# Layer-norm boundaries of an encoder trunk: the work of GpSimd handed to VectorE, tile by tile

## The chip, the cores and the metric

The kernel runs on one core of a Trainium2 chip. The metric is the device time of one execution in microseconds (us). TensorE (PE in the profile) multiplies matrices, with PEld for its weight loads; VectorE (DVE), ScalarE (ACT) and GpSimd (POOL) do elementwise work, each in the order of its own queue; SyncE (SP) issues all transfers.

## What is computed

The reference is a trunk of two layers on a sequence of 512 tokens of width 1024. Layer 0 mixes with gated linear attention, layer 1 with softmax attention; each layer then has an MLP of width 4096 with squared ReLU. After each of the four sub-layers stands the step that this document is about:

```
u = x * (1.0 + sc1) + sh1
y = gla_mixer(u, ...)                     # or chunk_attention, or squared_relu_mlp
x = layer_norm(DEEPNORM_ALPHA * x + (1.0 + g1) * y, ln_g[i, 0], ln_b[i, 0])
...
def layer_norm(x, g, b):
    mu = jnp.mean(xf, -1, keepdims=True)
    var = jnp.mean(jnp.square(xf - mu), -1, keepdims=True)
    return ((xf - mu) * lax.rsqrt(var + LN_EPS)) * g + b
```

`sh`, `sc` and `g` come from a conditioning vector and are columns per feature.

## The kernel before

Activations lie with features on the 128 partitions and tokens along the row: `xs[0..7]` are eight tiles of 128 features by 512 tokens, in fp32. Every large product is done with operands split in two (`hi`, rounded, and `lo`, the remainder `raw - hi`), three matmuls for one (`mm3`). ScalarE casts `hi`, and `lo_of` makes the remainder: 128x1024 for a weight tile (`emit_unit`), on VectorE for weights of kind `w` and `f`, on GpSimd for kinds `p` and `F`. There are two `p` tiles (one in each MLP) and two `F` tiles (first MLP weights of layer 1). `fill` and `fill_f` emit these units from a list `plan`; they take their places in the queues where they are emitted. All operations of one engine keep the order in which the program emits them (class `InOrder`), so each queue is an order written by hand. Line 47 is the helper that records every operation, so all rows of the trace name that line and groups are told apart by their tiles.

`boundary(...)` ends a sub-layer. It is called four times: after the linear attention (first), after the MLP of layer 0 (second, with `vfill`: the product behind it is the value projection of the attention), after the attention (third, in which the events hold no `"shift"`; called late here), and after the last MLP (fourth, `final`, which writes the output). Its stages:

1. Output tiles 0 to 3 of the sub-layer's last product are finished on all 512 tokens and evicted into `xs` (`ev`). A rough mean of the tokens (`shift_mm`, a matmul with `ones_h`, and a copy by ScalarE) is subtracted from all eight tiles, to keep the sum of squares small. In the first, second and fourth boundaries this lies ahead of the last tile; in the third behind the first half of tile 4.
2. `start_acc` sums tiles 0 to 3 in `accz` and their squares in `accq`.
3. Tiles 4 to 7 are computed in two halves of 256 tokens: `half_mm` is eight steps of three matmuls of 128x256; `half_ev` evicts, squares on ScalarE and adds to `accz` and `accq`. The order on TensorE is the first half of tiles 4 to 7, then the second half of tile 4 (in the third boundary also three steps of tile 5), then the statistics of the first half, then the rest.
4. `stats1` multiplies the sums by `ones_c` (which gives mean and mean square on all partitions), forms the variance, and centres the tiles; `stats2` finishes the inverse root `y`.
5. `ap1` scales a pair of tiles by `y` and applies the affine columns of the next sub-layer twice, once rounded (`un`, part 0) and once in fp32 (`us`); `ap2` makes the remainder (`un`, part 1). In the last boundary `norm` and `affine` do this and the output transfers follow.
6. The next product (`fg` with four weight tiles, or `v_mm`) goes through its eight steps, one for each tile of `un`, first half and then second half. The statistics of the second half stand behind the first two steps (three in the third boundary).

Between VectorE and GpSimd the elementwise work is shared so:

```
for j in (4, 5, 6, 7):
    if j > 5 or "shift" in events:
        tt(G, xs[j], xs[j], shift, ALU.subtract)
...
for k in (1, 3, 5, 7):
    tt(G, xs[k][:, hs], xs[k][:, hs], mn, ALU.subtract)
...
for k in (1, 3, 7) if final and hf else (1, 3, 5, 7):
    tt(G, xs[k][:, hs], xs[k][:, hs], y, ALU.mult)
```

GpSimd also adds most of the squares and makes the affine columns `a1`, `b1`, `ag`, `ab` (`ln_cols`).

Of the kernel before, what the change touches and what calls it, by code (L numbers as in the profile page):

```python
# [59 lines left out]
def trunk(ctx, tc, xT, c, ada, cols, gk1, gk2, w_qk, w_v, w_g, w_go, a_qk, a_v, a_tab,  # L60
# [128 lines left out]
    def emit_unit():  # L189
# [26 lines left out]
        lo_of(G if kind in "pF" else V, lo, raw, hi)  # L216
# [90 lines left out]
    def ln_cols(l, i, nxt):  # L307
# [4 lines left out]
        if nxt is not None:  # L312
            nl, sh, sc = nxt
            mS = mods[:, nl, sc * 8:sc * 8 + 8]
            mH = mods[:, nl, sh * 8:sh * 8 + 8]
            a1 = const.tile([P, 8], F32, name=nm("a1"))
            b1 = const.tile([P, 8], F32, name=nm("b1"))
            tt(G, a1, g, mS, ALU.mult)
            tt(G, b1, b, mS, ALU.mult)
            tt(G, b1, b1, mH, ALU.add)  # L320
            ag = const.tile([P, 8], F32, name=nm("ag"))
            ab = const.tile([P, 8], F32, name=nm("ab"))
            G.tensor_scalar(out=ag, in0=g, scalar1=ALPHA, scalar2=None, op0=ALU.mult)
            G.tensor_scalar(out=ab, in0=b, scalar1=ALPHA, scalar2=None, op0=ALU.mult)
            r.update(a=a1, b1=b1, ag=ag, ab=ab)
# [4 lines left out]
    def boundary(src, l, gt, open_lnt, mk_cols, fg_evac, events=None, final=False, vfill=None):  # L330
# [25 lines left out]
        def ev(m):  # L356
            stt(xs[m], pss[m], mod(l, gt, m), xs[m], ALU.mult, ALU.add)
            if m == 1:
                tt(V, accz, xs[0], xs[1], ALU.add)

        def shift_mm():
            pm = bank()
            T.matmul(pm, ones_h, accz, start=True, stop=True)
            A.copy(out=shift, in_=pm)
            for j in (4, 5, 6, 7):
                if j > 5 or "shift" in events:
                    tt(G, xs[j], xs[j], shift, ALU.subtract)
                else:
                    tt(V, xs[j], xs[j], shift, ALU.subtract)
            for j in (0, 1):  # L370
                tt(V, xs[j], xs[j], shift, ALU.subtract)

        events = events or [(0, range(8)), (1, range(8)), (2, range(8)), "shift", (3, range(8))]
        late = "shift" not in events
        for e in events:
            if e == "shift":
                shift_mm()
                continue
# [5 lines left out]
            if left[m] == 0:  # L384
                ev(m)
                if m < 3 and "shift" in events:
                    fill(3)
        lnc = mk_cols()
# [3 lines left out]
        def start_acc():  # L392
            for m in (2, 3):
                tt(V, xs[m], xs[m], shift, ALU.subtract)
            tt(V, accz, xs[0], xs[1], ALU.add)
            A.activation(out=accq, in_=xs[0], func=AF.Square)
            tt(G if "shift" in events else V, accq, accq, sq_of(xs[1], S), ALU.add)
            for m in (2, 3):
                tt(V, accz, accz, xs[m], ALU.add)
                if late and m == 3:  # L400
                    q = shift
                    A.activation(out=q, in_=xs[m], func=AF.Square)
                else:
                    q = sq_of(xs[m], S)
                tt(G, accq, accq, q, ALU.add)

        if "shift" in events:
            start_acc()
        else:
            fill_f(4)  # L410
# [6 lines left out]
        def half_ev(m, hf, ps, j, mid=lambda: None):  # L417
            hs = slice(hf * HT, (hf + 1) * HT)
            xh = xs[m][:, hs]
            stt(xh, ps[:, j * HT:(j + 1) * HT], mod(l, gt, m), xh, ALU.mult, ALU.add)  # L420
# [5 lines left out]
            tt(V if m == 7 or (final and hf) else G, accq[:, hs], accq[:, hs], q, ALU.add)  # L426
# [6 lines left out]
        def stats1(hf, last=None, fill_in=None):  # L433
# [13 lines left out]
            mn = tl("mn", 1)  # L447
            A.copy(out=mn, in_=dm)
            ve = tl("ve", 1)
            stt(ve, qm, LN_EPS, d2, ALU.add, ALU.subtract)  # L450
            tt(V, xs[0][:, hs], xs[0][:, hs], dm, ALU.subtract)
            for k in (1, 3, 5, 7):
                tt(G, xs[k][:, hs], xs[k][:, hs], mn, ALU.subtract)
# [4 lines left out]
            for k in (2, 4):  # L458
                tt(V, xs[k][:, hs], xs[k][:, hs], dm, ALU.subtract)
            st[hf] = dm, ve, y0  # L460

        def stats2(hf):
            hs = slice(hf * HT, (hf + 1) * HT)
# [3 lines left out]
            tt(V, xs[6][:, hs], xs[6][:, hs], dm, ALU.subtract)  # L467
# [3 lines left out]
            st[hf] = y  # L471
            for k in (1, 3, 7) if final and hf else (1, 3, 5, 7):
                tt(G, xs[k][:, hs], xs[k][:, hs], y, ALU.mult)
# [4 lines left out]
        def ap1(hf, p):  # L478
            ks = (2 * p, 2 * p + 1)
            hs = slice(hf * HT, (hf + 1) * HT)  # L480
            k = ks[0]
            tt(V, xs[k][:, hs], xs[k][:, hs], st[hf], ALU.mult)
            for k in ks:
                xh = xs[k][:, hs]
                a1, b1 = lnc["a"][:, k:k + 1], lnc["b1"][:, k:k + 1]
                us[k] = tl("u", 4)
                A.activation(out=un[k][:, 0, hs], in_=xh, func=AF.Identity, scale=a1, bias=b1)
                if k % 2:
                    V.tensor_scalar(out=us[k], in0=xh, scalar1=a1, scalar2=b1, op0=ALU.mult, op1=ALU.add)
                else:  # L490
                    A.activation(out=us[k], in_=xh, func=AF.Identity, scale=a1, bias=b1)

        def ap2(hf, p):
            hs = slice(hf * HT, (hf + 1) * HT)
            for k in (2 * p, 2 * p + 1):
                lo_of(V, un[k][:, 1, hs], us[k], un[k][:, 0, hs])

        def norm(hf, k):
            hs = slice(hf * HT, (hf + 1) * HT)
            tt(V, xs[k][:, hs], xs[k][:, hs], st[hf], ALU.mult)  # L500
# [20 lines left out]
        for m in range(4, 8):  # L521
            pa[m] = bank()
            half_mm(m, 0, pa[m], 0)
            if m == 4 and "shift" not in events:
                shift_mm()
                start_acc()
            half_ev(m, 0, pa[m], 0)
        pb = {m: bank() for m in range(4, 8)}
        half_mm(4, 1, pb[4], 0)
        if late:  # L530
            half_mm(5, 1, pb[5], 0, range(3))
            half_ev(4, 1, pb[4], 0)
            stats1(0)
            half_mm(5, 1, pb[5], 0, range(3, KT))
            stats2(0)
        else:
            stats1(0)
            stats2(0)
# [759 lines left out]
```

## Time and profile before

| | |
|---|---|
| median of three runs | 1222.27 us (1222.24 to 1222.6) |
| the profiled execution | 1222.72 us, of which the span of the instructions is 1220.9 us |
| TensorE busy | 1181.6 us, 97% of the span |
| VectorE busy | 831.1 us, 68% |
| ScalarE busy | 544.8 us, 45% |
| GpSimd busy | 176.6 us, 14% |
| mean granted clock of TensorE | 0.990 |
| share of the chain that ended last | TensorE 77%, VectorE 13%, ScalarE 4%, GpSimd 3% |

Matmuls are pipelined and their ends are modelled, so a busy TensorE is not one at its peak; the waits ahead of its instructions say more. In the timelines a row has the start, the time from the start of the first to the end of the last of the merged instructions, the engine, the operation with its output and inputs, their number, and in brackets how long the engine was idle before it and what ended that. A granted clock of 1.00 is 2.4 GHz, 0.50 is 1.2 GHz.

### The profile page before, as it was taken

Reading aid. Unit: us, or ns where it says so; the run is one execution under the profiler, and the core shown is the slowest. Engines: PE = TensorE matmul, PEld = TensorE weight load, DVE = VectorE, ACT = ScalarE, POOL = GpSimd, SP = SyncE. Lnnn points to the kernel's source line nnn. Section 1 sums busy time; section 2 is a strip of 40 time slices with the busy share of each in tenths; the row PEclk is TensorE's granted clock in tenths of the full one; section 3 lists DMA queues with packets and bytes.
Section 4 is the critical chain, followed back from the end, with each engine's and each line's share of the span. In section 5 each row is a group of like instructions: output and inputs, shape, how many; then the busy total and the mean of one; then the engine's idle time right before and its main releaser. Section 6 shows DMA issues by size and latency. Waiting matters only on the chain.

```text
span 1220.9 us, 15202 instructions
## 1 busy us (share of the span) xinstructions
PE 1181.6 (97%) x5742; PEld 985.9 (81%) x5742; DVE 831.1 (68%) x1260; ACT 544.8 (45%) x853; POOL 176.6 (14%) x189
## 2 busy tenths in 40 slices
PE   9999999899999999999899999998999999999995
PEld 5888888788888888888788786678888888888885
DVE  6788589777676677658834878898764443443467
ACT  4564545474243342342536656654641422322324
POOL 1000003610000000005511222235200000000035
PEclk9999999999999999999999999999899999999998
DMA  9756435028889889844026431321155232332201
GB/s 350 257 187 218 170 104 188 3 76 306 291 302 344 295 301 336 297 157 156 31 74 224 155 118 63 130 85 55 62 196 152 90 104 86 102 105 88 94 10 69
DMA packets 58282, 196.33 MB, mean 161 GB/s; under 512 B 6561, under 2 KB 10913, under 8 KB 58210
## 3 DMA queue, kind: packets, MB, share of 16 engines
q1 hardware_dynamic: 58210, 195.37, 46.1%
q8 instruction: 45, 0.74, 0.2%
q14 instruction: 27, 0.22, 0.1%
HBM read 174.37 MB, written 20.97 MB: 160 GB/s over the span
## 4 chain that ended last, share of the span: by engine, by line
PE 77%; DVE 13%; ACT 4%; POOL 3%; issue 2%; ACTq 0%; DVEq 0%; POOLq 0%
PE ps L47 76%; DVE af L47 5%; DVE x L47 3%; ACT af L47 2%; DVE ar L47 2%; POOL af L47 1%; DVE u L47 1%; POOL x L47 1%; DVE wlo L47 1%; PE warm L47 1%; ACT ar L47 1%; DVE d L47 1%; DVE y L47 1%; DVE t L47 0%; DVE raw L47 0%
## 5 line engine op out<-in xcount | busy, mean ns | idle before, releaser
L47 PE MATMUL ps<-ar,whi 128*128 128x512 f32 (+1 forms) x2880 | 822.1, 373 | 0.2 <-DVE ar L47 0.2
L47 PEld LDWEIGHTS ps<-ar,whi 128*128 128x128 f32 x2880 | 526.7, 190 | 96.4 <-issue 2.4
L47 PE MATMUL ps<-ar,wlo 128*128 128x512 f32 (+1 forms) x1440 | 526.0, 372 | 0.2 <-DVE wlo L47 0.2
L47 PEld LDWEIGHTS ps<-ar,wlo 128*128 128x128 f32 x1440 | 273.3, 190 | 46.9 <-DVE wlo L47 0.8
L47 ACT CAST whi<-raw 128x1024 fp32r<-128x1024 f32 (+1 forms) x169 | 169.5, 1010 | 204.8 <-PE ps L47 168.6
L47 DVE TENSOR_TENSOR wlo<-raw,whi 128x1024 fp32r<-128x1024 f32 x160 | 200.2, 1256 | 20.9 <-ACT whi L47 19.1
L47 DVE SCALAR_TENSOR_TENSOR x<-ps,mods,x 128x512 f32<-128x512 f32 (+1 forms) x96 | 63.0, 657 | 123.1 <-PE ps L47 123.1
L47 POOL TENSOR_TENSOR x<-x,af 128x512 f32<-128x512 f32 x14 | 25.4, 1843 | 808.7 <-ACT af L47 808.7
L47 DVE TENSOR_TENSOR h<-r 128x512 f32<-128x512 f32 (+1 forms) x72 | 49.2, 688 | 85.5 <-ACT r L47 84.7
L47 ACT ACTIVATE r<-ps 128x512 f32<-128x512 f32 (+1 forms) x72 | 39.1, 549 | 133.0 <-PE ps L47 132.8
L47 DVE SCALAR_TENSOR_TENSOR raw<-raw,csil 128x1024 f32<-128x1024 f32 x80 | 96.8, 1217 | 0.0
L47 PE MATMUL ps<-ar,fhi 128*128 128x256 f32 (+1 forms) x320 | 70.9, 317 | 6.8 <-DVE ar L47 5.9
L47 DVE TENSOR_TENSOR ar<-h,ar 128x512 fp32r<-128x512 f32 (+1 forms) x72 | 45.6, 633 | 39.5 <-ACT ar L47 38.4
L47 ACT CAST ar<-h 128x512 fp32r<-128x512 f32 (+1 forms) x72 | 41.2, 572 | 51.0 <-DVE h L47 51.0
L47 PEld LDWEIGHTS ps<-ar,fhi 128*128 128x128 f32 x320 | 53.9, 198 | 10.6 <-DVE ar L47 7.1
L47 PE MATMUL ps<-whi,ar 128*128 128x512 f32 x192 | 60.6, 390 | 0.0
L47 POOL PARTITION_ALL_REDUCE mb<-af x16 | 31.7, 1984 | 131.0 <-DVE af L47 123.9
L47 PE MATMUL ps<-ar,flo 128*128 128x256 f32 (+1 forms) x160 | 49.9, 312 | 0.0
L47 ACT ACTIVATE af<-x 128x256 f32<-128x256 f32 (+1 forms) x48 | 22.7, 486 | 57.6 <-POOL af L47 31.8
L47 PEld LDWEIGHTS ps<-whi,ar 128*128 128x128 f32 x192 | 36.0, 188 | 7.6
L47 ACT CAST fhi<-raw 128x1024 fp32r<-128x1024 f32 x30 | 31.4, 1049 | 23.7 <-DMA raw<-a_qk 12.2
L47 ACT ACTIVATE af<-af 128x1024 f32<-128x1024 f32 (+2 forms) x48 | 32.0, 698 | 20.9 <-DVE af L47 20.4
(149 smaller groups left out, 1139.4 us busy)
## 6 DMA issues: line engine op xcount, KB each, us to landing
raw<-f SPq DMA_DIRECT2D x128, 512.0 KB, 4.3
raw<-ada SPq DMA_DIRECT2D x80, 512.0 KB, 4.6
hraw<-ada SPq DMA_DIRECT2D x16, 512.0 KB, 9.0
raw<-a_qk SPq DMA_DIRECT2D x16, 512.0 KB, 5.4
khi_q<-fhi SPq DMA_DIRECT2D x14, 512.0 KB, 3.6
klo_q<-flo SPq DMA_DIRECT2D x14, 512.0 KB, 4.9
whi<-khi_q SPq DMA_DIRECT2D x14, 512.0 KB, 3.3
wlo<-klo_q SPq DMA_DIRECT2D x14, 512.0 KB, 4.3
```

The lines of the kernel that those rows point to most:

```text
L47: r = f(*a, **k)
```

## The change

All elementwise work of the boundaries goes to VectorE, and the orders are rewritten.

- The four weight remainders of kinds `p` and `F`, and the affine columns, go to VectorE; the columns are made at the start of `boundary` instead of behind its events.
- The shift is taken from tile 0 alone, twice its value, instead of from tiles 0 and 1; the sum of the two drops out of the evictions. In the third boundary the shift's product moves ahead of the last steps of tile 3, and the subtractions stay late: tiles 4 and 0 to 3 before the eviction of tile 4, the others each before its own.
- In the other three, tiles 4 to 7 and 0 to 2 are shifted before the eviction of tile 3, and tile 3 after it.
- `accq` is summed on VectorE throughout, with the squares of ScalarE in two buffers (one in the third boundary).
- The copy `mn` of the mean to SBUF drops out; all centring reads the mean from PSUM (`cen`). In the three inner boundaries the first statistics stand in the middle of the eviction of tile 4's second half, in the third without the three steps of tile 5 ahead of them.
- Centring, scaling, affine pieces and remainders are emitted one tile after the other (`cen`, `ap`, `lo`) instead of in pairs; the fp32 affine piece of the odd tiles moves from VectorE to ScalarE.
- The statistics of the second half stand behind three steps of the next product everywhere. In the second boundary the four weight tiles of the value projection's other half are all made after the first half's work.

```diff
-        lo_of(G if kind in "pF" else V, lo, raw, hi)
+        lo_of(V, lo, raw, hi)
...
-            tt(G, a1, g, mS, ALU.mult)
+            tt(V, a1, g, mS, ALU.mult)
...
+        lnc = mk_cols()
...
-            T.matmul(pm, ones_h, accz, start=True, stop=True)
-            A.copy(out=shift, in_=pm)
+            T.matmul(pm, ones_h, xs[0], start=True, stop=True)
+            A.activation(out=shift, in_=pm, func=AF.Copy, scale=2.0)
...
             if e == "shift":
                 shift_mm()
+                if not late:
+                    sub(4, 5, 6, 7, 0, 1, 2)
...
             A.activation(out=accq, in_=xs[0], func=AF.Square)
+            q = [shs[:, 1, :], shs[:, 1 if late else 0, :]]
+            for m in (1, 2, 3):
+                A.activation(out=q[m % 2], in_=xs[m], func=AF.Square)
+                tt(V, accz, xs[0] if m == 1 else accz, xs[m], ALU.add)
+                tt(V, accq, accq, q[m % 2], ALU.add)
...
+            if late:
+                if m == 4:
+                    sub(4, 0, 1, 2, 3)
+                    start_acc()
+                else:
+                    sub(m)
+            half_ev(m, 0, pa[m])
...
+        def ap(hf, *ks):
             hs = slice(hf * HT, (hf + 1) * HT)
             for k in ks:
                 xh = xs[k][:, hs]
                 a1, b1 = lnc["a"][:, k:k + 1], lnc["b1"][:, k:k + 1]
                 us[k] = tl("u", 4)
+                tt(V, xh, xh, st[hf][1], ALU.mult)
                 A.activation(out=un[k][:, 0, hs], in_=xh, func=AF.Identity, scale=a1, bias=b1)
+                A.activation(out=us[k], in_=xh, func=AF.Identity, scale=a1, bias=b1)
...
+        half_ev(4, 1, pb[4], lambda: stats1(0, 2))
+        stats2(0)
+        half_mm(5, 1, pb[5], 0)
+        ap(0, 0, 1)
+        lo(0, 0)
+        half_ev(5, 1, pb[5])
+        cen(0, 2, 3)
+        ap(0, 2)
+        lo(0, 1)
...
+        def second():
+            ap(0, 5)
+            lo(0, 4)
+            stats1(1, 2)
+            cen(0, 6, 7)
+            ap(0, 6)
+            lo(0, 5)
+            stats2(1)
+            ap(0, 7)
+            lo(0, 6, 7)
+
+        def third():
+            ap(1, 0, 1)
+            for k in range(2, KT):
+                cen(1, k)
+                ap(1, k)
+                lo(1, k - 2)
+            lo(1, KT - 2, KT - 1)
```

In the last boundary the order is rewritten likewise, with a centring and a scaling in front of each affine piece:

```diff
+            norm(1, 3)
+            affine(1, 3, (3, 6))
+            cen(1, 4)
             norm(1, 4)
             affine(1, 4, (4, 5))
+            cen(1, 5)
             norm(1, 5)
             affine(1, 5, (4, 5))
+            cen(1, 6)
             norm(1, 6)
-            affine(1, 3, (3, 6), True)
             affine(1, 6, (3, 6), True)
+            cen(1, 7)
+            norm(1, 7)
             affine(1, 7, (7,))
```

## Rows read from the trace of the kernel before

**Rows 1.** Waits of TensorE: us in total, times, longest.

```profile
PE ps L47 <- DVE af L47: 12.6, 9, 3.8
PE ps L47 <- DVE ar L47: 9.3, 8, 2.3
```

**Rows 2.** Timeline of TensorE, first boundary.

```profile
218.74 0.70 PE L47 MATMUL ps<-af,ones_c 128*128 128x256 f32 x2 [0.54 <-DVE af L47]
223.24 1.22 PE L47 MATMUL ps<-af,ones_c 128*128 128x256 f32 x2 [3.81 <-DVE af L47]
...
249.78 0.39 PE L47 MATMUL ps<-ar,fhi 128*128 128x256 f32 x1 [1.56 <-DVE ar L47]
...
261.27 0.63 PE L47 MATMUL ps<-ar,whi 128*128 128x512 f32 x2
```

**Rows 3.** Stretches: busy us (x instructions) by engine, granted clock, DMA share, GB/s.

```profile
core 0: us, PE busy (x) PEld busy (x) DVE busy (x) ACT busy (x) POOL busy (x), PEclk, DMA share, GB/s
223.24:226.20 2.96, 2.96 (x12) 2.78 (x13) 1.02 (x4) 1.18 (x4) 0.97 (x2) 0.50 0.01 3
584.20:588.00 3.80, 3.80 (x17) 3.69 (x18) 2.24 (x7) 1.48 (x4) 2.19 (x3) 0.55 0.00 0
...
249.80:255.80 6.00, 6.00 (x50) 6.00 (x51) 4.82 (x12) 5.03 (x10) 1.29 (x1) 1.00 0.01 3
861.80:867.80 6.00, 6.00 (x28) 6.00 (x29) 4.83 (x12) 5.03 (x10) 1.29 (x1) 0.50 0.00 0
```

**Rows 4.** Groups by shape: busy us, mean ns of one; idle before, releaser.

```profile
L47 POOL TENSOR_TENSOR x<-x,mn 128x256 f32<-128x256 f32 x32 | 25.6, 829 | 26.0 <-ACT mn L47 26.0
...
L47 DVE TENSOR_TENSOR mods<-mods,col 128x8 f32<-128x8 f32 x8 | 1.3, 167 | 0.3
```

**Rows 5.** Timeline of VectorE, first boundary.

```profile
210.75 1.29 DVE L47 TENSOR_TENSOR x<-x,af 128x512 f32<-128x512 f32 x2
...
215.47 0.47 DVE L47 SCALAR_TENSOR_TENSOR x<-ps,mods,x 128x256 f32<-128x256 f32 x1
215.97 0.42 DVE L47 TENSOR_TENSOR af<-af,x 128x256 f32<-128x256 f32 x1
...
229.81 0.95 DVE L47 TENSOR_TENSOR x<-x,y 128x256 f32<-128x256 f32 x1
...
249.98 0.41 DVE L47 TENSOR_TENSOR x<-x,y 128x256 f32<-128x256 f32 x1
250.32 0.40 DVE L47 TENSOR_SCALAR u<-x,a,b 128x256 f32<-128x256 f32 x1
```

**Rows 6.** Timeline of ScalarE, first boundary.

```profile
201.09 0.59 ACT L47 COPY af<-ps 128x512 f32<-128x512 f32 x1 [0.46 <-PE ps L47]
...
251.43 1.08 ACT L47 ACTIVATE ar<-x,b,a 128x256 fp32r<-128x256 f32 x2
```

**Rows 7.** Timeline of VectorE, second boundary.

```profile
562.51 2.32 DVE L47 TENSOR_TENSOR wlo<-raw,whi 128x1024 fp32r<-128x1024 f32 x1
```

**Rows 8.** Timeline of TensorE, second boundary.

```profile
582.35 0.70 PE L47 MATMUL ps<-af,ones_c 128*128 128x256 f32 x2 [0.96 <-DVE af L47]
584.19 0.85 PE L47 MATMUL ps<-af,ones_c 128*128 128x256 f32 x2 [1.15 <-DVE af L47]
...
629.87 0.39 PE L47 MATMUL ps<-whi,ar 128*128 128x512 f32 x1
```

**Rows 9.** Timeline of VectorE, ahead of the third boundary's half tiles.

```profile
809.18 3.50 DVE L47 TENSOR_TENSOR wlo<-raw,whi 128x1024 fp32r<-128x1024 f32 x3
...
818.00 1.40 DVE L47 SCALAR_TENSOR_TENSOR x<-ps,mods,x 128x512 f32<-128x512 f32 x2
```

**Rows 10.** Timeline of TensorE, third boundary.

```profile
835.51 0.70 PE L47 MATMUL ps<-af,ones_c 128*128 128x256 f32 x2 [2.99 <-DVE af L47]
...
861.78 0.58 PE L47 MATMUL ps<-ar,fhi 128*128 128x256 f32 x1 [2.34 <-DVE ar L47]
...
875.96 0.63 PE L47 MATMUL ps<-ar,whi 128*128 128x512 f32 x2
```

**Rows 11.** Timeline of SyncE's queue, end of the kernel.

```profile
1217.48 0.45 SPq L516 DMA_DIRECT2D out<-af  x1
```

More of the change, by code (lines that the diff above doesn't have):

```diff
@@ L385, in boundary @@
                 ev(m)
-                if m < 3 and "shift" in events:
+                if m < 3 and not late:
                     fill(3)
-        lnc = mk_cols()
         lnt = open_lnt()
@@ L392, in start_acc @@
         def start_acc():
-            for m in (2, 3):
-                tt(V, xs[m], xs[m], shift, ALU.subtract)
-            tt(V, accz, xs[0], xs[1], ALU.add)
             A.activation(out=accq, in_=xs[0], func=AF.Square)
[L397 to L407, printed above, removed]
+            q = [shs[:, 1, :], shs[:, 1 if late else 0, :]]
[4 more added lines that the diff above has]
+        if late:
+            fill_f(4)
+        else:
+            sub(3)
             start_acc()
-        else:
-            fill_f(4)
         def half_mm(m, hf, ps, j, ks=range(KT)):
@@ L431, in tl, with cen, stats1 @@
             return lnt.tile([P, HT], F32, tag=tag, bufs=bufs, name=nm(tag))
-        def stats1(hf, last=None, fill_in=None):
+        def cen(hf, *ks):
+            hs = slice(hf * HT, (hf + 1) * HT)
+            for k in ks:
+                tt(V, xs[k][:, hs], xs[k][:, hs], st[hf][0], ALU.subtract)
+        def stats1(hf, n0, last=None, fill_in=None):
             hs = slice(hf * HT, (hf + 1) * HT)
@@ L523, in boundary @@
             half_mm(m, 0, pa[m], 0)
[L524 to L527, printed above, removed]
+            if late:
+                if m == 4:
+                    sub(4, 0, 1, 2, 3)
+                    start_acc()
+                else:
+                    sub(m)
+            half_ev(m, 0, pa[m])
         pb = {m: bank() for m in range(4, 8)}
         half_mm(4, 1, pb[4], 0)
[L530 to L534, printed above, removed]
+        if final:
+            stats1(0, 4)
             stats2(0)
[L536 to L539 removed]
+            half_ev(4, 1, pb[4], lambda: norm(0, 0))
             half_mm(5, 1, pb[5], 0)
[L541 removed]
+            affine(0, 0, (0, 2))
+            cen(0, 4, 5)
+            norm(0, 1)
             affine(0, 1, (1, 3))
[L543 to L544 removed]
+            half_ev(5, 1, pb[5], lambda: norm(0, 2))
             half_mm(6, 1, pb[6], 0)
+            affine(0, 2, (0, 2))
+            norm(0, 3)
             affine(0, 3, (1, 3))
[L547 to L548 removed]
+            cen(0, 6, 7)
+            half_ev(6, 1, pb[6], lambda: norm(0, 5))
             half_mm(7, 1, pb[7], 0)
             affine(0, 5, (5, 7))
+            norm(0, 7)
+            affine(0, 7, (5, 7))
             def fill_in():
@@ L622, in boundary @@
             fg(0, fa, range(n))
-            ap1(0, 3)
-            ap2(0, 2)
-            stats1(1)
-            ap2(0, 3)
-            stats2(1)
-            fg(0, fa, range(n, 8))
-            ap1(1, 0)
-            for p in range(1, 4):
-                ap1(1, p)
-                ap2(1, p - 1)
-            ap2(1, 3)
+            second()
+            fg(0, fa, range(n, 8))
+            third()
             fb = [bank(), bank()]
@@ L1241, in trunk @@
     evac_h, run = mlp_fns()
-    u = boundary(o, 1, G1, opener(es, 1), lambda: ln_cols(1, 0, (1, SH2, SC2)), evac_h, ev)
+    u = boundary(o, 1, G1, opener(es, 1), lambda: ln_cols(1, 0, (1, SH2, SC2)), evac_h, ev, late=True)
     hs = run(u, 1)
```

108 lines of the change are left out of this document (33 added, 75 removed).

## The prediction, made before the changed kernel was run

> **What bounds the kernel now.** I read the waits of TensorE first, then TensorE's timeline through the four boundaries (first about 190 to 262 us, second 562 to 630, third 813 to 876, last 1175 to the end), then VectorE, ScalarE and GpSimd in the same stretches. Outside the boundaries TensorE issues without a gap worth naming; all its waits on VectorE together are 12.6 and 9.3 us [rows 1], so the change has to earn its time there. In the first boundary TensorE has nothing left after 218.2 (218.74 less its wait) but the two statistics products and what depends on them: it waits 0.54 us for the sum, then 3.81 us for the sum of squares, later 1.56 us for the first tile of the second half, and leaves the boundary at 261.27 [rows 2]. The long wait costs twice: up to 226.20 the granted clock is 0.50, the lower level of 1.2 GHz, where it is 1.00 from 249.80 on; after the 2.34 us wait of the third boundary it is 0.50 from 861.80 to 867.80, six microseconds at half rate [rows 3, 10].
>
> Who is late? GpSimd takes 829 ns for a subtraction on 256 columns [rows 4]; VectorE does such a piece in 0.41 us and starts the next 0.34 us after it (249.98 to 250.32), and two pieces of 512 columns in 1.29 us, so one every 0.61 [rows 5]. While GpSimd runs, VectorE is slowed as well: the multiplication that has 0.41 us at 249.98 has 0.95 us at 229.81, and the next instruction starts 0.87 later [rows 5]; a 1024-column remainder has 2.32 us at 562.51 against three in 3.50 us at 809.18 [rows 7, 9].
>
> **The sum, boundary by boundary.** Unit prices, all from stretches without GpSimd: 512-column two-operand instruction 0.61 start to start; 256-column one 0.34; a dependent one 0.45 to 0.50 (215.47 to 215.97); 1024-column remainder 1.135, as three end 3.50 us after the first starts and one has 1.22 [rows 5, 9]; ScalarE 0.49 for each affine piece of 256 columns (two in 1.08) [rows 6]. A half product is 24 matmuls at 0.12 us (50 in 6.00 us [rows 3]), 2.88 us; a step of the following product is 12 of them, 1.44; a pair of statistics products 0.93. For a signal between engines I take 0.05.
>
> *First boundary.* The shift is ready when ScalarE's copy ends, 201.09 + 0.59 [rows 6]. VectorE then has in its order: seven subtractions 7 x 0.61 = 4.27; the eviction of tile 3, 0.66; three remainders 3.41; the subtraction of tile 3, 0.61; three sums and three sums of squares 3.66 and 0.19 of waiting for a square: 214.5. Each of the four half evictions costs 0.50 + 0.49 (sum, and the wait for ScalarE's square) + 0.34 = 1.33; the last sum is there at 219.41 and the last sum of squares at 219.90. TensorE is free at 218.2, so it waits 1.3 us instead of 0.54 and 3.81, and the product of tile 5 starts at 220.4, where it now starts after 223.24 and at half rate. I take the clock as staying at 1.00, because it did after the 1.56 us wait [rows 2, 3]. The inverse root follows: square of the mean, variance, logarithm and exponential at some 0.4 us each and three dependent multiplications at 0.45 end at 223.8. TensorE goes through tiles 5 to 7 (8.64), three steps (4.32) and the second statistics (0.93) until 234.3. The order now costs three small waits: ScalarE does two affine pieces per tile where VectorE did one of them, so its square of the second mean starts only after tile 5, at 235.5; variance, four centrings, one scaling follow on VectorE, and the remainder of tile 5 ends at 238.3, 1.08 us after TensorE wants it. Tile 6 is 0.49 late, the first tile of the second half 0.34. After that VectorE needs 3 x 0.34 and ScalarE 2 x 0.49 per tile against TensorE's 1.44, and TensorE never waits. Exit: 254.93 against 261.27, **-6.3**.
>
> *Second.* VectorE starts the subtractions at 562.51 + 1.135 = 563.64 [rows 7]; the same list gives the sums at 581.3 and 581.8, and TensorE is free at 581.4 (582.35 less 0.96): it waits 0.1 instead of 0.96 and 1.15 [rows 8], and the stretch at 0.55 of the clock behind them goes [rows 3]. The remainders of tiles 5 and 6 are 1.31 and 0.56 late; the four weight remainders, now queued in one lump ahead of the second half, make the first of them 0.28 late. Exit 626.95 against 629.87 [rows 8]: **-2.9**.
>
> *Third.* Here VectorE is the bound. The five column products of the affine coefficients move to its queue in the attention phase; such an instruction has 167 ns [rows 4]; bounds 0, if a wait behind them swallows it, and 5 x 0.167 = 0.84; I take 0.6, as that stretch is VectorE's own. The last two evictions start at 818.00 in the trace [rows 9], held up by a sum of tiles 0 and 1 that the change drops; I let them end at 818.0, with the 0.6 at 818.6. The remainders of the four weight tiles that were shared with GpSimd are all VectorE's: 4 x 1.135 = 4.54, to 823.3; five subtractions 3.05; six sums 3.66 and 0.38 of waiting, since one buffer holds all the squares; then 1.33 for tile 4 and 1.33 + 0.72 for each of 5, 6, 7, whose subtraction now stands in front. The last sum comes at 837.5. The three steps of tile 5 that stood ahead of the statistics (nine matmuls, 1.08) now stand behind, so TensorE is free at 832.0 (835.51 - 2.99 - 1.08 + 0.6). It waits 5.5 us, against 2.99 [rows 10] and 0.34 more, and runs about 3.3 us at half rate (bounds 2.96 and 6.0, the stretches of [rows 3]; nearer the first, whose wait of 3.81 us is nearer), reaching the next product at 848.7 instead of 846.1. There it waits 0.32, 0.49 and 0.34, and the 2.34 us wait with its six microseconds at half rate is gone. Exit 873.86 against 875.96 [rows 10]: **-2.1**.
>
> *Last.* No product follows, so the tail is VectorE's own. GpSimd did four of the second half's eight centrings and three of its scalings beside it; now each of the last four tiles costs 0.34 + 0.45, in series. The variance comes at 1209.1 instead of 1208.8, the last scaling ends at 1217.6, the last affine piece at 1218.3, and the last output transfer starts about 0.85 us later than at 1217.48 [rows 11]: **+0.8** (bounds 0 and 1.5).
>
> *Nothing paid for:* the coefficient products of the other boundaries fall into VectorE's idle time before the first eviction (0.9 us and more); the two remainders of kind p run when VectorE's boundary work is done, some 4 us before TensorE leaves the boundary; without that cover 1.1 us each. ScalarE's scaled copy replaces a plain one of 0.59 [rows 6]. No transfer is added or moved; staging buffers come free earlier than behind GpSimd.
>
> Together -6.3 - 2.9 - 2.1 + 0.8 = -10.5 us. The profiled execution took 1222.72 (span 1220.9), 0.45 above the median of 1222.27; from the median this is **1211.8 us**.
>
> **What the sum hangs on.** Everything is proportional to VectorE's pace. Redoing the three lists with every VectorE piece 5% quicker gives -13.4 in total, 5% slower -7.1, 10% slower -2.0, and at 15% (0.39 instead of 0.34) +1.4.
>
> **A rule against it.** Consecutive instructions in [rows 5] start 0.34 us apart at 0.41 us each, and 0.61 apart at 0.68: they overlap. The Trainium skill, VectorE: DVE Perf Modes, section The DRAIN you can't avoid, says that the next instruction does not start until the pipeline has emptied, though it adds that an instruction that is not held starts earlier. By its first half the sum would be that of rival (b), by the rows it is the one above.
>
> **The rivals.**
> (a) *The clock falls anyway* (chance 0.16). The second boundary lost its clock after waits of 0.96 and 1.15 us with one product between [rows 3, 8], so a wait of 1.3 may be enough in the first: about 2.9 us lost if six microseconds run at half rate. In the third the longer figure of [rows 3] costs 1.2 more. Total -6.4: 1215.9. Against it: the 1.00 after 1.56 us.
> (b) *Pieces don't overlap* (0.08): full durations 0.41 and 0.68. The three lists give -1.0, the tail +0.8: 1222.1, no change. Against it stand the starts in [rows 5]; for it, that many of the new pieces wait for a neighbour engine and could lose the overlap.
> (c) *Slower* (0.05): VectorE's long durations come not from GpSimd but from the boundary's other traffic. Then a scaling stays at the 0.87 from start to start that the 0.95 us one shows, in all three lists: about +51 us, 1273. It decides from a pace of about 0.38 on, where the change is worth nothing. Against it: from 249.98 GpSimd is idle, ScalarE and TensorE are busy as before, and the price is 0.34.
> The forecast itself has 0.68; 0.03 is left to what I don't see.
>
> **Numbers.** The forecast's own range is 1208.9 to 1215.2 (pace 5% either way); (a) widens it to 1217, and a third boundary without the second loss of clock and a quicker VectorE to 1206.5. A difference under 0.2%, 2.4 us, can't be told from none: faster 0.86, same 0.08, slower 0.06.
>
> **What would show it.** Right: GpSimd's busy time falls from 176.6 us to about 50; 256-column scalings at 0.42 us throughout; TensorE's waits near 0.2 to 1.4 us at the first two statistics, but a longer one, about 5 us, in the third boundary; exits some 6, 9 and 11 us earlier than before; no half rate in the first two boundaries; the tail after the last matmul about a microsecond longer. Wrong: pieces at 0.6 us or more with GpSimd idle; a wait of TensorE over 2 us inside the eight steps of a following product; a third boundary whose exit gives back more than the first gained.

## The result and the profile of the changed kernel

The changed kernel takes **1212.32 us** (median of 4 runs, 1211.67 to 1213.36) against 1222.26 us for the kernel before beside it: ratio 0.9919, interval 0.9902 to 0.9936. The forecast was 1211.8 us, range 1206.5 to 1217.0. The profiled execution took 1211.67 us, 0.65 below its own median, and that of the kernel before 0.45 above its own, so the difference between the two traces (spans 1220.9 and 1209.8, 11.1 us) is 1.2 us over the 9.9 us of the medians.

First the busy time on the page, and the waits of TensorE that answer to [rows 1]:

```profile
PE 1177.0 (97%) x5742; PEld 981.0 (81%) x5742; DVE 827.5 (68%) x1359; ACT 555.0 (46%) x870; POOL 49.1 (4%) x61
```

```profile
PE ps L47 <- DVE af L47: 7.6, 3, 5.5
...
PE ps L47 <- DVE ar L47: 7.2, 10, 1.6
```

GpSimd went from 176.6 us to 49.1, and the two waits from 21.9 us to 14.8. Most of the rest of the gain is clock: TensorE is busy 4.6 us less with the same number of matmuls. TensorE's timeline, which answers to [rows 2, 8, 10], shows where:

```profile
200.41 1.02 PE L47 MATMUL ps<-x,ones_h 128*128 128x512 f32 x2
...
219.88 1.21 PE L47 MATMUL ps<-af,ones_c 128*128 128x256 f32 x4 [1.30 <-DVE af L47]
...
238.66 0.38 PE L47 MATMUL ps<-ar,fhi 128*128 128x256 f32 x1 [0.78 <-DVE ar L47]
...
255.26 0.63 PE L47 MATMUL ps<-ar,whi 128*128 128x512 f32 x2
...
575.40 1.21 PE L47 MATMUL ps<-af,ones_c 128*128 128x256 f32 x4
...
594.13 0.73 PE L47 MATMUL ps<-fhi,ar 128*128 128x512 f32 x2 [0.73 <-DVE ar L47]
...
620.76 0.39 PE L47 MATMUL ps<-whi,ar 128*128 128x512 f32 x1
...
828.46 2.08 PE L47 MATMUL ps<-af,ones_c 128*128 128x256 f32 x4 [5.54 <-DVE af L47]
...
864.71 0.63 PE L47 MATMUL ps<-ar,whi 128*128 128x512 f32 x2
```

And the granted clock behind those waits, as in [rows 3]:

```profile
core 0: us, PE busy (x) PEld busy (x) DVE busy (x) ACT busy (x) POOL busy (x), PEclk, DMA share, GB/s
219.88:226.00 6.12, 6.12 (x47) 5.86 (x48) 4.71 (x13) 2.79 (x7) 0.00 (x0) 1.00 0.01 3
575.40:581.00 5.60, 5.60 (x43) 5.33 (x43) 4.64 (x12) 2.26 (x6) 0.00 (x0) 1.00 0.01 1
828.46:832.20 3.74, 3.74 (x13) 3.38 (x14) 2.45 (x7) 1.52 (x5) 0.00 (x0) 0.50 0.00 0
832.30:838.00 5.70, 5.70 (x49) 5.70 (x49) 4.71 (x14) 2.42 (x6) 0.00 (x0) 1.00 0.00 0
```

The first statistics wait 1.30 us in the first boundary, not at all in the second, and the clock stays at 1.00 behind both. In the third they wait 5.54 us, longer than the 2.99 of [rows 10], and the half rate that follows lasts 3.74 us; the second loss of clock, behind 2.34 us in [rows 10], is gone.

To compare stretches I cut each trace at the start of the shift's product in the first boundary (200.03 before, 200.41 after: a head 0.38 us longer, which belongs to no edit: the runs below have between 200.21 and 200.82 there), at the three exits, and at the end of the span (spans are read to 0.1 us):

| us | shift to exit 1 | exit 1 to 2 | exit 2 to 3 | exit 3 to end |
|---|---|---|---|---|
| before | 61.24 | 368.60 | 246.09 | 344.94 |
| after | 54.85 | 365.50 | 243.95 | 345.09 |
| difference | **-6.4** | **-3.1** | **-2.1** | **+0.15** |
| forecast | -6.3 | -2.9 | -2.1 | +0.8 |

### The profile page after: what moved, and what is told of

Read it like the earlier page. It is cut to its first block, busy times and chain, and to the rows that moved or that the text cites. A ratio compares the mean times of both kernels' runs of the same rounds, so it can differ in the third digit from the quotient of the medians.

```text
span 1209.8 us, 15107 instructions
## 1 busy us (share of the span) xinstructions
PE 1177.0 (97%) x5742; PEld 981.0 (81%) x5742; DVE 827.5 (68%) x1359; ACT 555.0 (46%) x870; POOL 49.1 (4%) x61
## 4 chain that ended last, share of the span: by engine, by line
PE 77%; DVE 15%; ACT 6%; issue 2%; DMA 0%; DVEq 0%; ACTq 0%
PE ps L47 76%; DVE af L47 6%; DVE x L47 4%; ACT af L47 3%; ACT ar L47 1%; DVE wlo L47 1%; DVE ar L47 1%; PE warm L47 1%; ACT u L47 1%; DVE d L47 1%; DVE flo L47 1%; DVE t L47 0%; DVE y L47 0%; DVE raw L47 0%; DMA raw<-f 0%
## 5 line engine op out<-in xcount | busy, mean ns | idle before, releaser
L47 DVE TENSOR_TENSOR wlo<-raw,whi 128x1024 fp32r<-128x1024 f32 x162 | 197.2, 1223 | 23.3 <-ACT whi L47 21.2
L47 DVE TENSOR_TENSOR h<-r 128x512 f32<-128x512 f32 (+1 forms) x72 | 45.2, 633 | 79.1 <-ACT r L47 78.2
L47 ACT ACTIVATE ar<-x,b,a 128x256 fp32r<-128x256 f32 x48 | 28.6, 595 | 25.8 <-DVE x L47 25.8
L47 PE MATMUL ps<-af,vt 128*128 128x512 f32 (+3 forms) x128 | 36.9, 436 | 2.0 <-ACT af L47 2.0
```

Source lines behind the costliest of these rows:

```text
L47: r = f(*a, **k)
```

## The experiments

All were timed beside the kernel before. The table has every run, cut in the same way; the sections below say what each tells apart.

| run | median us | ratio to before, interval | shift to exit 1 | 1 to 2 | 2 to 3 | 3 to end |
|---|---|---|---|---|---|---|
| e0_again (changed kernel) | 1211.89 | 0.9919, 0.9905 to 0.9932 | 54.82 | 365.44 | 243.80 | 345.13 |
| e1_engine | 1224.13 | 1.0016, 1.0007 to 1.0025 | 59.98 | 369.41 | 246.56 | 346.78 |
| e2_share | 1214.61 | 0.9938, 0.9926 to 0.9951 | 55.85 | 367.25 | 243.91 | 345.94 |
| e3_beside | 1217.33 | 0.9961, 0.9949 to 0.9974 | 56.99 | 366.97 | 246.03 | 345.32 |
| e8_head | 1216.59 | 0.9952, 0.9940 to 0.9965 | 58.05 | 366.73 | 244.23 | 344.87 |
| e5_ahead | 1211.51 | 0.9914, 0.9900 to 0.9928 | 54.84 | 365.48 | 243.95 | 345.18 |
| e6_fin3 | 1211.74 | 0.9916, 0.9903 to 0.9930 | 54.82 | 365.44 | 244.83 | 345.10 |
| e4_cols | 1211.56 | 0.9915, 0.9902 to 0.9929 | 54.82 | 365.44 | 243.28 | 345.14 |
| b1_list | 1209.67 | 0.9902, 0.9887 to 0.9917 | 53.96 | 364.57 | 243.01 | 345.14 |
| b2_third | 1207.99 | 0.9890, 0.9873 to 0.9906 | 53.95 | 364.57 | 241.21 | 345.11 |
| b3_last | 1205.88 | 0.9872, 0.9858 to 0.9887 | 53.96 | 364.56 | 241.61 | 343.66 |

e0_again is the standard.

> The changed kernel itself, unaltered, as the standard for the runs beside it. 1212.3 us, exits of the three inner boundaries at 255.3, 620.8 and 864.7 us.

### Engine or order?

e1_engine gives VectorE all the work and leaves the order; e2_share leaves the new order and gives GpSimd its share back.

```diff
 # e1, on the kernel before (and likewise for shift, weights, columns, squares)
-                tt(G, xs[k][:, hs], xs[k][:, hs], mn, ALU.subtract)
+                tt(V, xs[k][:, hs], xs[k][:, hs], mn, ALU.subtract)
 # e2, on the changed kernel (and likewise for cen and norm)
-                tt(V, xh, xh, st[hf][1], ALU.mult)
+                tt(G if k % 2 else V, xh, xh, st[hf][1], ALU.mult)
...
-            tt(V, accq[:, hs], accq[:, hs], q, ALU.add)
+            tt(V if m == 7 or (final and hf) else G, accq[:, hs], accq[:, hs], q, ALU.add)
```

> The kernel before with nothing changed but the engine: every elementwise instruction of GpSimd in the boundaries, the weight remainders and the affine columns goes to VectorE in the place in which it stood; order, shift and the copy of the mean stay as they were. My theory (the gain comes from the order made for VectorE, since GpSimd's pieces, put into VectorE's list as they stand, are in front of what TensorE waits for): with the unit prices of the prediction the first exit comes at -2.0 us, the second at -2.3, the third at -1.7 (cumulative), the whole at about 1220.5 us; the waits of 3.81 and 1.15 us for the sum of squares go, but new ones of 2 to 3 us for the remainder of tile 0 come, since its scaling stands behind eight centrings, four scalings and two evictions. Rival (the engine is the gain, the order is worth little): at least three quarters of the gain, 1215 us or less.

> The changed kernel's order with GpSimd's share given back: the sums of squares except that of tile 7, and centring and scaling of the odd tiles, with the mean copied to SBUF for it. The shift, the weight remainders and the affine columns stay on VectorE. My theory (a GpSimd piece takes 0.83 us and slows VectorE's pieces beside it from one in 0.34 us to one in 0.87): TensorE waits again 3 us or more for the first sum of squares in the first boundary, the exits are no earlier than before, the whole is 1219 to 1226 us. Rival (the gain is the order, not the engine): 1215 us or less.

On VectorE alone, the old order is no faster than before: 1224.13 us, 0.16% slower. On the same engine the new order (with its shift from one tile, the mean read from PSUM and the odd affine pieces on ScalarE) saves some 12 us. e1_engine's lists show why: first VectorE in the first boundary, then TensorE.

```profile
223.01 1.43 DVE L47 TENSOR_TENSOR x<-x,mn 128x256 f32<-128x256 f32 x4
...
226.59 1.43 DVE L47 TENSOR_TENSOR x<-x,y 128x256 f32<-128x256 f32 x4
...
232.62 0.75 DVE L47 TENSOR_TENSOR ar<-u,ar 128x256 fp32r<-128x256 f32 x2
```

```profile
220.36 1.21 PE L47 MATMUL ps<-af,ones_c 128*128 128x256 f32 x4 [1.92 <-DVE af L47]
...
233.09 0.58 PE L47 MATMUL ps<-ar,fhi 128*128 128x256 f32 x1 [2.36 <-DVE ar L47]
```

The 3.81 us wait of [rows 2] has not gone, as I expected, but fallen to 1.92; and the four odd centrings and four odd scalings that GpSimd did beside VectorE now stand in front of the first remainders: 232.62, and TensorE waits 2.36 us for them (2 to 3 us expected). My expectation for the whole was 3.6 us too low. Counted from the shift, the exits come 1.3, 0.5 and 0 us earlier where I expected 2.0, 2.3 and 1.7, and another 1.8 us is the last boundary (346.78 against 344.94), for which the expectation has no change.

e2_share went against me. I expected 3 us or more of waiting at the first sum of squares and 1219 to 1226 us; it waits 0.22 and 0.34 us there and takes 1214.61. In the new order the engine is worth only about 2.7 us. So the sharing itself was not what made the sums late; but the shift's subtractions and the affine columns stay on VectorE in this run, and the next section turns to them.

### What was late in GpSimd's queue

Back to the kernel before: the timeline of GpSimd in the first boundary.

```profile
201.83 7.92 POOL L47 TENSOR_TENSOR x<-x,af 128x512 f32<-128x512 f32 x4 [195.00 <-ACT af L47]
209.71 1.19 POOL L47 TENSOR_TENSOR a<-col,mods 128x8 f32<-128x8 f32 x1
...
213.44 1.82 POOL L47 TENSOR_TENSOR af<-af,af 128x512 f32<-128x512 f32 x1
...
220.33 2.33 POOL L47 TENSOR_TENSOR af<-af,af 128x256 f32<-128x256 f32 x3 [0.53 <-ACT af L47]
```

Four subtractions take 7.92 us, the affine columns 3.7 us more, and only at 213.44 does the first sum of squares begin. e8_head takes that head alone, on the kernel before:

```diff
-            tt(G, a1, g, mS, ALU.mult)
+            tt(V, a1, g, mS, ALU.mult)
...
-                if j > 5 or "shift" in events:
-                    tt(G, xs[j], xs[j], shift, ALU.subtract)
-                else:
-                    tt(V, xs[j], xs[j], shift, ALU.subtract)
+                tt(V, xs[j], xs[j], shift, ALU.subtract)
```

> The kernel before, with only the head of GpSimd's queue taken over by VectorE: the shift's subtractions of tiles 4 to 7 (7.92 us on GpSimd in the first boundary) and the affine columns (3.7 us behind them). Sums of squares, centring and scaling stay shared, in the order of before. My theory after the first four runs (what was late was GpSimd's first sum of squares, because of what stood ahead of it in its queue; that part of the gain needs no new order): the sums of squares begin some 5 us earlier, the 3.81 us wait falls below 1 us, the half rate behind it goes, first exit -3.5 to -4.9 us, second another -2 to -2.8, third 0 to -1: 1214 to 1216.5 us. Rival (the tile by tile order makes the gain): 1219 us or more.

GpSimd in e8_head now begins with the sums of squares, and TensorE's first statistics follow (the second fence):

```profile
206.72 1.28 POOL L47 TENSOR_TENSOR af<-af,af 128x512 f32<-128x512 f32 x1 [199.94 <-ACT af L47]
212.99 1.55 POOL L47 TENSOR_TENSOR af<-af,af 128x512 f32<-128x512 f32 x1 [4.98 <-ACT af L47]
```

```profile
220.62 1.13 PE L47 MATMUL ps<-af,ones_c 128*128 128x256 f32 x4 [1.46 <-DVE af L47]
```

The first sum starts 6.7 us earlier, the waits of 0.54 and 3.81 us become one of 1.46, the clock from there to 223.6 is 1.00 (0.50 in [rows 3]), and the kernel takes 1216.59 us: 5.4 of the 10 us from taking over about a quarter of what GpSimd gave up (its busy time is 143.3 us here, 176.6 before, 49.1 after). That is just outside the 1214 to 1216.5 us that I expected, and so is every stretch: -3.2, -1.9 and -1.9 us for -3.5 to -4.9, -2 to -2.8 and 0 to -1. Of the third's 1.9 us, some 1.5 (an estimate, half of the difference) are clock and not the head of the queue: behind the same 2.34 us wait the half rate lasts 3.0 us here (856.68 to 859.70) and six in [rows 3]. Handing over the remaining work without a new order loses it again (e1_engine, +7.5 us from here); with one it brings another 4.7.

### Does GpSimd slow VectorE, whoever waits for it?

```diff
             st[hf] = dm, y
+            if not final:
+                tt(G, gs, gs, y[:, 0:P], ALU.subtract)
+                for _ in range(19):
+                    tt(G, gs, gs, gs, ALU.subtract)
```

> The changed kernel with extra GpSimd work that nothing waits for: behind each inverse root of the three inner boundaries GpSimd does 20 subtractions of 128x128 on a tile of its own, some 8 us in a row by half the 829 ns of a 256-column piece. My theory (GpSimd at work slows VectorE, whoever waits for it): VectorE's 256-column pieces in these stretches go from 0.42 to about 0.9 us, TensorE waits 1 to 2 us for the second statistics and some 3 us within the steps of the second half, so +4 to +5 us a boundary, 1222 to 1230 us in all. Rival (GpSimd costs only where its own result is waited for): no change, 1212 us, VectorE's pieces at 0.42 us.

It took 1217.33, 5.4 us more than the standard: the effect is real, but 1.5 to 2.2 us in each of the three boundaries and not 4 to 5. The queues of GpSimd and VectorE in the second half of the first boundary:

```profile
241.40 9.81 POOL L47 TENSOR_TENSOR gs<-gs 128x128 f32<-128x128 f32 x19
```

```profile
243.63 0.41 DVE L47 TENSOR_TENSOR x<-x,ps 128x256 f32<-128x256 f32 x1
244.07 0.65 DVE L47 TENSOR_TENSOR x<-x,y 128x256 f32<-128x256 f32 x1
244.65 0.61 DVE L47 TENSOR_TENSOR ar<-u,ar 128x256 fp32r<-128x256 f32 x1
```

Not every piece is slowed: the centring, which reads the mean from PSUM, keeps its 0.41 us; scaling and remainder, with both operands in SBUF, have 0.65 and 0.61. VectorE's groups by shape (busy us, mean ns of one) say the same of the kernel before, and then of the changed one, where GpSimd is idle beside them:

```profile
L47 DVE TENSOR_TENSOR x<-x,y 128x256 f32<-128x256 f32 x33 | 18.8, 579 | 0.2
...
L47 DVE TENSOR_TENSOR x<-x,ps 128x256 f32<-128x256 f32 x32 | 11.8, 411 | 0.0
```

```profile
L47 DVE TENSOR_TENSOR x<-x,y 128x256 f32<-128x256 f32 x64 | 26.2, 421 | 0.9
L47 DVE TENSOR_TENSOR x<-x,ps 128x256 f32<-128x256 f32 x64 | 24.3, 414 | 0.0
```

The Trainium skill, SBUF — State Buffer, section Who interferes with whom, has this: an instruction of VectorE with two inputs in SBUF contends with a GpSimd instruction that reads SBUF, one with at most one such input (outside the two-port modes) does not. These rows agree. But the number of tiles that an instruction reads from SBUF does not settle it alone: the affine piece on VectorE in the kernel before, with one tile and two columns, has 0.40 us in [rows 5] and twice that beside GpSimd. Whether it is a case of the Trainium skill's exception no row shows.

```profile
230.68 0.83 DVE L47 TENSOR_SCALAR u<-x,a,b 128x256 f32<-128x256 f32 x1
```

### Is a wait of TensorE a cost? Three edits on the third boundary

e5_ahead fills the 5.5 us wait with the second half of tile 5. e6_fin3 takes a 1.59 us wait away that lies just before the boundary. e4_cols moves the affine columns to where VectorE waits.

```diff
 # e5
+        if late:
+            half_mm(5, 1, pb[5], 0)
         half_ev(4, 1, pb[4], lambda: stats1(0, 2))
         stats2(0)
-        half_mm(5, 1, pb[5], 0)
+        if not late:
+            half_mm(5, 1, pb[5], 0)
 # e6
-            fill(5)
             fin3(7)
+            fill(5)
 # e4
+        def mid():
+            if late:
+                lnc.update(mk_cols())
+            stats1(0, 2)
```

> The changed kernel, with one edit in the third boundary: the second half of tile 5 (2.88 us on TensorE) stands ahead of the first statistics, where TensorE waits 5.5 us, and not behind them. My theory (the third boundary is bound by VectorE to its end, so TensorE's wait is only where the slack shows): the wait falls to 2.6 us, the half rate behind it shrinks, and the same time comes back as waits for remainders within the eight steps (about 0.8, 0.6 and 1.7 us); the exit stays within 0.5 us of 864.71, the whole within 0.7 us of 1212.3. Rival (the wait is the cost): the exit 2.9 us earlier, and up to 1.9 more where the half rate goes too: 1207.5 to 1209.5 us.

> The changed kernel; ahead of the third boundary the last remainder of the attention's output (0.75 us on VectorE), for which TensorE waits 1.59 us, stands ahead of three weight remainders (3.5 us) and not behind them. My theory (the third boundary is bound by VectorE's list from here to its exit, so what closes gaps in it, 0.82, 0.81 and 0.17 us, moves the exit by as much): TensorE's 1.59 us wait goes, the first statistics and the exit come 1.5 to 1.9 us earlier, 1210.6 us. Rival (TensorE only waits longer for the statistics): exit unchanged, 1212.3 us.

> The changed kernel; the affine columns of the third boundary are made in its middle, where VectorE waits for the square of the mean, and not ahead of it in the attention, where five instructions of 128x8 took from 772.20 to 773.58 us. My theory (the term of +0.6 us of the prediction): the third exit comes 0.5 to 0.7 us earlier, 1211.7 us. Rival (VectorE's later waits swallow them anyway): exit within 0.2 us.

TensorE in e5_ahead:

```profile
828.66 2.05 PE L47 MATMUL ps<-af,ones_c 128*128 128x256 f32 x4 [2.74 <-ACT af L47]
...
840.83 0.39 PE L47 MATMUL ps<-ar,fhi 128*128 128x256 f32 x1 [0.54 <-DVE ar L47]
...
848.22 0.39 PE L47 MATMUL ps<-ar,fhi 128*128 128x256 f32 x1 [1.36 <-DVE ar L47]
```

The wait halves, the half rate shortens, and all of it comes back as waits for remainders; the stretch is 243.95 us (243.80 in the standard). Filling the longest wait of the changed kernel gains nothing: with TensorE relieved, VectorE's list sets the exit.

e6_fin3 missed: its stretch is 244.83, 1.0 us longer than the standard's (in the median, 1211.74, it is no slower). VectorE's and TensorE's lines there, and the clock behind the first statistics (columns as in [rows 3]):

```profile
801.25 0.75 DVE L47 SCALAR_TENSOR_TENSOR ar<-af,col,ar 128x512 fp32r<-128x512 f32 x1 [0.79 <-ACT ar L47]
802.19 3.50 DVE L47 TENSOR_TENSOR wlo<-raw,whi 128x1024 fp32r<-128x1024 f32 x3 [0.18 <-ACT whi L47]
```

```profile
806.52 1.12 PE L47 MATMUL ps<-x,ones_h 128*128 128x512 f32 x2 [1.61 <-DVE x L47]
```

```profile
828.24:834.40 6.16, 6.16 (x25) 5.81 (x26) 4.64 (x12) 2.07 (x5) 0.00 (x0) 0.50 0.00 0
```

Moving the call moved ScalarE's part as well: its casts now stand behind the piece that waits for VectorE, VectorE waits 0.79 and 0.18 us for ScalarE, the weight remainders start at 802.19 instead of 800.36 in the standard, and TensorE's 1.59 us wait reappears as 1.61 for the shift's product. So nothing was gained up to the first statistics: they stand 207.57 us behind the second exit, 207.59 in the standard, after a wait of 5.51 us (5.53). The microsecond lost is clock: the half rate behind that wait lasts 6.16 us here and 3.74 in the changed kernel. What the gaps in VectorE's list are worth was not tested by this edit; b2_third does it. But it shows that from the first statistics on VectorE is not the only bound: relieving TensorE gains nothing (e5_ahead), and a slower TensorE moves the exit.

e4_cols gives 0.5 us (243.28 against 243.80), the prediction's 0.6: TensorE's wait at this place of the attention falls from 1.13 us in the standard to 0.64, and the first statistics come 207.10 us behind the second exit instead of 207.59. The size had another cause than the 167 ns of [rows 4]. In the changed kernel's attention phase, GpSimd and then VectorE:

```profile
772.45 1.78 POOL L47 PARTITION_ALL_REDUCE mb<-af  x1 [2.78 <-DVE b L47]
```

```profile
772.27 0.16 DVE L47 TENSOR_TENSOR b<-col,mods 128x8 f32<-128x8 f32 x1
772.47 1.04 DVE L47 TENSOR_TENSOR b<-b,mods 128x8 f32<-128x8 f32 x1
```

This eight-column product takes 1.04 us because GpSimd's reduction starts beside it: in e4_cols, with GpSimd idle, it takes 0.17. Two more of the five are slowed as well, and the last ends with the reduction, at 774.26 (not at 773.58, as the expectation read it).

### Versions that beat both

If VectorE's list binds, filling its gaps must bring every exit forward. b1_list moves three instructions in the inner boundaries, b2_third adds e4_cols and a mended e6_fin3, b3_last rewrites the last boundary's list.

```diff
 # b1
             lo(0, 4)
-            stats1(1, 2)
             cen(0, 6, 7)
-            ap(0, 6)
             lo(0, 5)
+            stats1(1, 2)
+            ap(0, 6)
 # b2: remainders of fill(5) held back, ScalarE's casts left in place
+            state["hold"] = []
             fill(5)
+            los.extend(state["hold"])
+            state["hold"] = None
             fin3(7)
+            los.pop(0)()
+            los.pop(0)()
 # b3, in part
+            cen(1, 4)
             norm(1, 3)
             affine(1, 3, (3, 6))
-            cen(1, 4)
+            cen(1, 5)
             norm(1, 4)
```

> The changed kernel with three instructions moved in the second half's list of the three inner boundaries: the centrings of tiles 6 and 7 and the remainder of tile 5 stand ahead of the second variance, where VectorE waited 0.83 us for ScalarE's square, and not behind it. Nothing is left out. My theory (in the changed kernel VectorE's list binds every inner boundary, so what fills a gap in it brings the exit forward, also in the third, where TensorE's waits behind the second statistics are only 0.24 us): each of the three exits comes 0.9 us earlier against the one before it, 2.7 us in all, about 1209.2 us. Rival (TensorE's remaining waits are the most there is): 1.0 in the first, 1.2 in the second, 0.2 in the third at most, and likely less, since the third has no slack to give.

> The kernel of b1_list, with the third boundary's affine columns in its middle (as in e4_cols), and the start of the third boundary mended as e6_fin3 did not: ScalarE keeps its order (three casts, then the attention's last piece), while VectorE takes that piece's remainder first, then two weight remainders, and the third one between the evictions of tiles 2 and 3. My theory (VectorE's list binds, so filling its gaps of 0.82, 0.81 and 0.17 us counts): third exit another 0.6 and 1.3 us earlier than in b1_list, about 1207.4 us. Rival (the casts, the shift or TensorE bind there): 0.6 us at most.

> The kernel of b2_third with the last boundary's list rewritten: what the second statistics don't need is moved behind what they need, or into the waits for the inverse root; each centring of the second half stands one scaling ahead of its own, so that no scaling waits for the centring just ahead of it; one of the two affine pieces on VectorE goes to ScalarE. My theory (from the last statistics on, the end is VectorE's list): the last transfer is issued some 1.8 us earlier, about 1205.6 us. Rival (the last transfers or ScalarE set the end): within 0.5 us of b2_third.

VectorE before the edit waited for the second variance (changed kernel), and works through it after (b1_list):

```profile
236.19 0.42 DVE L47 SCALAR_TENSOR_TENSOR ve<-ps,d 128x256 f32<-128x256 f32 x1 [0.83 <-ACT d L47]
```

```profile
235.69 0.75 DVE L47 TENSOR_TENSOR x<-x,ps 128x256 f32<-128x256 f32 x2
236.35 0.42 DVE L47 TENSOR_TENSOR ar<-u,ar 128x256 fp32r<-128x256 f32 x1
236.68 0.42 DVE L47 SCALAR_TENSOR_TENSOR ve<-ps,d 128x256 f32<-128x256 f32 x1
```

The stretches shorten by 0.86, 0.87 and 0.79 us against the standard. The third was to decide between theory and rival, and it does not: the 0.24 us of idle time that I counted there is not all by which TensorE was late, since the ends of its matmuls are modelled. The same four steps (tiles 5 to 7 and the first of the second half) in the changed kernel and then in b1_list, columns as in [rows 3]:

```profile
847.90:854.64 6.74, 6.46 (x51) 5.91 (x50) 5.71 (x16) 5.08 (x11) 0.00 (x0) 1.00 0.00 0
846.52:852.29 5.77, 5.77 (x51) 5.77 (x50) 4.80 (x13) 4.42 (x10) 0.00 (x0) 1.00 0.00 0
```

TensorE was 0.97 us late there, so the rival, rightly counted, allows 1.0 us. That VectorE's list binds is shown by e5_ahead, and for the part up to the first statistics by b2_third, whose first statistics are these:

```profile
825.08 2.07 PE L47 MATMUL ps<-af,ones_c 128*128 128x256 f32 x4 [5.70 <-DVE af L47]
```

They come 205.90 us behind the second exit (207.64 in b1_list) although TensorE waits longer for them than before, and the third stretch is another 1.8 us shorter (1.9 expected). b3_last, with the same list there, has 0.4 us more; its half rate lasts 4.91 us (824.59 to 829.50). It issues its last transfer 340.70 us after the third exit instead of 342.33: 1.6 us (1.8 expected). Together 1205.88 us, 15.4 below the kernel before.

## Why the prediction was right, point by point

- **First boundary, -6.3 (measured -6.4).** The wait of 1.3 us at the first statistics came as 1.30, and the clock stayed at 1.00. The idle time listed ahead of the late steps (0.78 and 0.23 us) looks like less than the 1.08, 0.49 and 0.34 forecast, but by the starts of the steps TensorE is 1.03, 0.49 and 0.29 us late: the four steps from tile 5 on take 7.57 us instead of 5.76 (columns as in [rows 3]).

```profile
237.62:245.19 7.57, 6.51 (x51) 5.91 (x50) 6.55 (x18) 5.22 (x11) 0.00 (x0) 1.00 0.01 2
```

- **Second, -2.9 (-3.1).** No wait at the statistics (0.1 forecast). By the starts of the steps TensorE is 1.02, 0.57 and 0.52 us late for 1.31, 0.56 and 0.28; the idle times listed are 0.73, 0.27 and 0.21.
- **Third, -2.1 (-2.1).** Wait 5.54 for 5.5; half rate 3.74 us for 3.3; 0.19, 0.49 and 0.30 us late within the steps for 0.32, 0.49 and 0.34; 0.5 of the 0.6 for the columns, by e4_cols. That VectorE binds it is shown by b2_third up to the first statistics; behind them it does in e5_ahead, but a longer half rate moves the exit too (e6_fin3). That the half rate came near the forecast is in part luck: I sized it by the length of the wait, and behind waits of 5.51 and 5.71 us it lasts 6.16 us (e6_fin3) and 4.91 (b3_last). In the trace with 6.16 the third boundary gains 1.3 us and not 2.1. The bounds that I gave for it, 2.96 and 6.0, were the better part of that term.
- **Last, +0.8 (+0.15).** The mis-sized term. VectorE's tail is as long as I said: the last transfer is issued 342.33 us after the third exit for 341.52 before, +0.81. But its landing, which I took as unchanged, became shorter: 2.34 us before, 1.74 after. The last two rows of the transfer queue, before and after:

```profile
1216.96 0.42 SPq L518 DMA_DIRECT2D out<-af  x1
1217.48 0.45 SPq L516 DMA_DIRECT2D out<-af  x1
```

```profile
1205.62 0.38 SPq L499 DMA_DIRECT2D out<-af  x1
1207.04 0.34 SPq L497 DMA_DIRECT2D out<-af  x1
```

The last transfer now starts 1.42 us after the one before it, where it was 0.52. In all seven further runs with this tail (e0_again, e3_beside, e4_cols, e5_ahead, e6_fin3, b1_list, b2_third) it lands in 1.74 to 1.75 us, and in the three with 0.52 to 0.55 us between the two (e1_engine, e2_share, e8_head) in 2.33 to 2.35; in b3_last, with 0.97 us between them, in 1.89. The transfer engines are idle from 1207.60 to 1207.85, just ahead of it, and in the kernel before never from 1217.45 to 1218.00. That the emptier queue is the reason fits all of these; no run changes the distance alone.
- **What it hangs on.** VectorE's pace was as taken: 421 ns a scaling, 414 a centring. The starts stay 0.34 us apart where pieces are independent, so rival (b), and with it the first half of the Trainium skill's rule that the prediction quotes, would have been wrong here by about 10 us; its addition, that an instruction which is not held starts earlier, fits. Rival (a) fell with the 1.00 behind 1.30 us, rival (c) with the 421 ns.
- **Where the reasoning was too simple.** "Who is late? GpSimd" named the engine, and the sum then charged the new lists piece by piece. The total came out, but the cause is narrower: the head of GpSimd's queue (5.4 us, e8_head), and for the rest the order, without which the change of engine is worth less than nothing (e1_engine) and with which it is worth 2.7 us (e2_share). The prediction offered no price for the order with the engines kept, which was the better question. e8_head and e2_share come near to one: both have the head on VectorE and share the rest, in the old order (1216.59) and in the new (1214.61). That makes some 5.4 us for the head, 2.0 for the order and 2.7 for the remaining work on VectorE, if done in this sequence; the last two are about as large as the intervals of these runs, and e2_share also has the weight remainders on VectorE.
- Not tried: the shift from one tile against two, the double buffer of the squares, the centring from PSUM and the odd affine pieces on ScalarE, each by itself.

## What to carry to other kernels

Before moving work off a late engine, look at what stands ahead of the late result in its queue: taking over that head may be half the gain. When one engine takes over everything, write its list by when each result is wanted, one tile at a time; the same instructions in the old order can cost more than they save. And test a wait by filling it before believing that it costs: filling the longest wait of TensorE here was worth nothing, and closing a 0.8 us gap in VectorE's list was worth 0.8 us in each of three boundaries. A stretch of one trace that holds a fall of the clock can be a microsecond off the next trace of the same list: look at the granted clock before crediting the edit.

## What the runs showed of the hardware

- Beside GpSimd, VectorE's 256-column instructions with both operands in SBUF go from 0.42 us to 0.61 to 0.65 (128x128 work on one tile, e3_beside) and to 0.95 in [rows 5]; an affine piece with one tile and two columns from 0.40 to 0.83 (kernel before); an eight-column product from 0.17 to 1.04 beside a reduction. A centring with one operand in PSUM stays at 0.41.
- The length of the wait alone does not say whether the clock falls. Behind 1.92 us at e1_engine's first statistics it is 1.00 from 220.36 to 223.00; behind 1.92 us in e2_share's second boundary it is 0.55 from 596.53 to 600.00; after 1.53 us in e1_engine's third boundary it is 1.00 from 847.99 to 851.00.
- Nor does it say how long the half rate lasts behind it: 3.74 us behind 5.54 us of waiting (changed kernel), 6.16 behind 5.51 (e6_fin3), 4.91 behind 5.71 (b3_last); six behind 2.34 us in [rows 3], 3.0 behind 2.34 in e8_head.
- The last output transfer of 128 KB lands in 1.74 us when it is issued 1.42 us behind the one before it, in 1.89 at 0.97 us and in 2.34 at 0.52 us.
